# Loading Q and K in 1 MB transfers of 512 B rows, in place of 512 KB transfers of 1 KB rows

## The chip, the cores and the metric

The kernel runs on one core of a Trainium2 chip; the other cores are idle. The metric is the device time of one execution in microseconds, fast runs compared with fast runs (a run is called slow when it lies over 1.5% above the fastest of the same kernel). Ratios are to the kernel before, measured beside each run on the same chip, with a 95% interval in brackets. A profiled execution is shown beside it: its span, from the first to the last instruction, is some 2 us shorter than the time of the execution.

## The reference

Cross-covariance attention over 8 x 12 heads of 512 tokens by 64 channels, all in float32. The attention matrix is 64 x 64 for each head, a product over the tokens:

```python
Q_norm = Q / (np.linalg.norm(Q, axis=-2, keepdims=True) + 1e-10)
K_norm = K / (np.linalg.norm(K, axis=-2, keepdims=True) + 1e-10)
attn = np.einsum('bhnd,bhne->bhde', Q_norm, K_norm)
attn = np.exp(attn - np.max(attn, axis=-1, keepdims=True))
attn = attn / (np.sum(attn, axis=-1, keepdims=True) + 1e-10)
return np.einsum('bhnd,bhde->bhne', V, attn)
```

Two facts matter here. Each of Q, K, V and the output is 12.58 MB, so 50.33 MB cross between HBM and SBUF whatever the kernel does. And Q and K enter only through a sum over tokens: any order of the tokens will do for them, if it is the same for both. The order of V is that of the output.

## The kernel before

A unit is four heads, and there are 24 units. Partition p owns tokens 4p to 4p+3 of each head, 1 KB in one piece (T = 4, D = 64, HU = 4). Every transfer has 512 KB, and all are issued by SyncE.

```python
Qf = Q.rearrange("b h (p t) d -> p (b h) t d", p=128)      # K, V and the output alike
qp = ctx.enter_context(tc.tile_pool(name="qp", bufs=5))    # for Q and K each; vp: 5
LOAD_AHEAD = 3
STORE_LAG = 6

def load_qk(u):
    qf[u] = qp.tile([128, HU, T, D], F32, name="qf")
    kf[u] = qp.tile([128, HU, T, D], F32, name="kf")
    nc.sync.dma_start(out=qf[u], in_=Qf[:, u * HU:(u + 1) * HU])
    nc.sync.dma_start(out=kf[u], in_=Kf[:, u * HU:(u + 1) * HU])
# ... load_v, store; casts to bf16 (VectorE), the products q.k, q.q and k.k of a head in one
#     128 x 128 block, norms, exp, the product with V ...
for u in range(LOAD_AHEAD):
    load_qk(u)
    load_v(u)
# ...
for s in range(U + 2):
    if s + LOAD_AHEAD < U:
        load_qk(s + LOAD_AHEAD)
        load_v(s + LOAD_AHEAD)
    if 0 <= s - STORE_LAG:
        store(s - STORE_LAG)
    # ... grams(s), norms(s), logits(s - 1), exps(s - 1), vtrans(s), casts(s + 1), outs(s - 2)
```

## Time and profile before

| | before |
|---|---|
| time, median of 2 runs | 144.87 us (144.48 to 145.25) |
| span of the profiled run | 143.1 us |
| moved by the DMA engines | 50.49 MB, 353 GB/s in the mean |
| VectorE, TensorE, ScalarE busy | 71%, 67%, 45% of the span |
| data packets | 49,152 of 1,024 B |

The prediction below shows the lines that carry this reading. In all such lines the span is cut into 40 slices, a digit of the DMA row is the busy share in tenths, and the engines are PE (TensorE's matmuls), PEld (its weight loads), DVE (VectorE), ACT (ScalarE), POOL (GpSimd) and SP (SyncE). A packet is one record of a DMA engine's work. One view more: the issues of transfers (what is written and read, the issuing queue, the count, the size, and the median time from issue to landing in us):

```profile
qf<-in_Q_dram SPq DMA_DIRECT2D x24, 512.0 KB, 8.3
kf<-in_K_dram SPq DMA_DIRECT2D x24, 512.0 KB, 8.4
vf<-in_V_dram SPq DMA_DIRECT2D x24, 512.0 KB, 8.4
out_dram<-so SPq DMA_DIRECT2D x24, 512.0 KB, 7.9
```

A transfer of 512 KB at 353 GB/s is 1.5 us of work, yet takes 8 us to land: by an estimate from these two (8.3 / 1.5) some five transfers queue ahead of it. The DMA engines always have work (9 tenths or more in 38 of the 40 slices), and the kernel goes at the pace of their packets.

### The profile page before, as it was taken

The page shows a single profiled execution, that of the slowest core. Times are in us where ns is not written, and L with a number is a line of the kernel's source. Part 1 is how long each engine was busy: PE and PEld are TensorE (multiplying, and loading weights), DVE is VectorE, ACT ScalarE, POOL GpSimd, SP SyncE. Part 2 cuts the span into 40 slices and gives each one's busy share as a digit, 9 for nine tenths or more (in the row PEclk, how much of TensorE's full clock was granted, in tenths as well). Part 3 has the DMA queues.
Part 4 walks back from the last instruction along what each step waited for, and adds up shares of the span by engine and source line. Part 5 has one row for each costly group of instructions (what it writes and reads, how often), then busy time and mean ns, then how long its engine had stood idle before and what let it go on. Part 6 is the DMA issues. An engine that isn't in the chain of part 4 may idle for free.

```text
span 143.1 us, 2715 instructions
## 1 busy us (share of the span) xinstructions
PE 95.3 (67%) x864; PEld 83.7 (59%) x864; DVE 100.9 (71%) x432; ACT 64.8 (45%) x193; POOL 29.9 (21%) x39
## 2 busy tenths in 40 slices
PE   0245879775896797686559874776795694397820
PEld 0234669664795686575557763765694683397620
DVE  0435888989888987696786886883868868767410
ACT  3003406764377644715706536437074273371840
POOL 6003302332033330311302303302022032031100
PEclk9999999999559856857975589655559559855555
DMA  4999999999999999999999999999999999999993
GB/s 133 336 353 349 348 348 351 350 348 348 348 350 348 376 370 378 368 371 384 368 372 380 372 376 379 371 380 371 375 369 369 371 382 372 382 377 386 377 322 113
DMA packets 50701, 50.49 MB, mean 353 GB/s; under 512 B 1536, under 2 KB 50688, under 8 KB 50688
## 3 DMA queue, kind: packets, MB, share of 16 engines
q1 hardware_dynamic: 50688, 50.34, 104.5%
q8 instruction: 6, 0.10, 0.3%
q14 instruction: 7, 0.06, 0.1%
HBM read 37.75 MB, written 12.58 MB: 352 GB/s over the span
## 4 chain that ended last, share of the span: by engine, by line
DMA 65%; DVE 14%; SPq 12%; PE 2%; ACT 1%; issue 1%; ACTq 0%
DMA vf<-in_V_dram 59%; DMA qf<-in_Q_dram 6%; SPq L65 5%; DVE vb L84 4%; SPq L66 4%; DVE ab L134 4%; SPq L70 3%; DVE scr L100 3%; DVE kqs L111 2%; PE lg L119 2%; ACT ex L125 1%; DVE rinv L131 1%; PE po L153 0%; ACT so L154 0%; DVE qkb L78 0%
## 5 line engine op out<-in xcount | busy, mean ns | idle before, releaser
L92 PE MATMUL gram<-qkb 128*128 128x128 bf16 x384 | 39.6, 283 | 20.0 <-DVE qkb L80 19.4
L105 POOL TENSOR_TENSOR rq<-nsq,mhalf 128x4 f32<-128x4 f32 x24 | 27.6, 1151 | 102.0 <-DVE nsq L100 102.0
L92 PEld LDWEIGHTS <-qkb 128*128 128x128 bf16 x384 | 33.8, 130 | 25.3 <-DVE qkb L80 24.6
L125 ACT ACTIVATE ex<-lg,rq 128x64 f32<-128x64 f32 x48 | 14.7, 310 | 63.2 <-PE lg L119 63.2
L119 PE MATMUL lg<-eye,kqs 128*128 128x64 f32 x96 | 22.8, 381 | 19.4 <-DVE kqs L111 19.3
L119 PEld LDWEIGHTS lg<-eye,kqs 128*128 128x128 f32 x96 | 18.8, 271 | 24.9 <-DVE kqs L111 24.9
L145 ACT COPY vt<-vps 128x512 bf16<-128x512 bf16 x48 | 25.7, 593 | 8.7 <-PE vps L143 8.7
L84 DVE CAST vb<-vf 128x1024 bf16<-128x1024 f32 x24 | 16.7, 694 | 15.2 <-DMA vf<-in_V_dram 15.2
L154 ACT COPY so<-po 128x512 f32<-128x512 f32 x48 | 26.4, 618 | 0.3 <-PE po L153 0.3
L143 PE MATMUL vps<-identb,vb 128*128 128x128 bf16 x192 | 20.9, 274 | 1.9 <-DVE vb L84 1.9
L153 PE MATMUL po<-ab,vt 128*128 128x128 bf16 x192 | 20.9, 274 | 0.6 <-DVE ab L134 0.6
L143 PEld LDWEIGHTS <-vb 128*128 128x128 bf16 x192 | 19.3, 138 | 2.2 <-DVE vb L84 2.2
L80 DVE CAST qkb<-kf 128x512 bf16<-128x512 f32 x24 | 10.2, 424 | 11.6 <-DMA kf<-in_K_dram 11.6
L153 PEld LDWEIGHTS <-vt 128*128 128x128 bf16 x192 | 17.4, 129 | 0.9 <-DVE ab L134 0.9
L134 DVE SCALAR_TENSOR_TENSOR ab<-ex,rinv,blocks 128x128 bf16<-128x128 f32 x48 | 14.7, 349 | 0.9
L111 DVE SCALAR_TENSOR_TENSOR kqs<-gram,rq,blocks 128x128 f32<-128x128 f32 x48 | 14.5, 344 | 0.0
L78 DVE CAST qkb<-qf 128x512 bf16<-128x512 f32 x24 | 10.2, 425 | 5.1 <-DMA qf<-in_Q_dram 5.1
L100 DVE CUSTOM_DVE_ANT_0 scr<-gram,swap 128x128 f32<-128x128 f32 x48 | 13.7, 286 | 0.0
L100 DVE CUSTOM_DVE_ANT_0 scr<-gram,ident 128x128 f32<-128x128 f32 x48 | 13.6, 284 | 0.0
L79 DVE CAST qkb<-qf 128x512 bf16<-128x512 f32 x24 | 10.1, 420 | 0.0
L81 DVE CAST qkb<-kf 128x512 bf16<-128x512 f32 x24 | 10.1, 419 | 0.0
L125 ACT ACTIVATION_READ_ACCUMULATOR ex<-lg,rq 128x1 f32 x48 | 9.4, 196 | 0.0
(18 smaller groups left out, 15.8 us busy)
## 6 DMA issues: line engine op xcount, KB each, us to landing
qf<-in_Q_dram SPq DMA_DIRECT2D x24, 512.0 KB, 8.3
kf<-in_K_dram SPq DMA_DIRECT2D x24, 512.0 KB, 8.4
vf<-in_V_dram SPq DMA_DIRECT2D x24, 512.0 KB, 8.4
out_dram<-so SPq DMA_DIRECT2D x24, 512.0 KB, 7.9
```

Source lines behind the costliest of these rows:

```text
L84: nc.vector.tensor_copy(w.rearrange("p t h d -> p h t d"), vf[u])
L92: nc.tensor.matmul(o, x, x, start=(t == 0), stop=(t == T - 1))
L100: nc.vector.tensor_tensor_reduce(out=scr, in0=blk, in1=m, scale=1.0, scalar=1e-20, op0=ALU.mult, op1=ALU.add, accum_out=n2[:, c, p:p + 1],)
L105: nc.gpsimd.tensor_tensor(out=r, in0=n2, in1=mhalf, op=ALU.pow)
L111: nc.vector.scalar_tensor_tensor(out=kk[:, p], in0=gram[u][:, p, 0::3, :], scalar=rq[u][:, 1, p:p + 1], in1=off_diag, op0=ALU.mult, op1=AL ...
L119: nc.tensor.matmul(l[:, p, :], kqs[u][:, p].rearrange("p a d -> p (a d)"), eye2)
L125: nc.scalar.activation(e[:, p, :], lg[u][:, p, :], AF.Exp, scale=rq[u][:, 0, p:p + 1], accum_out=s[:, p:p + 1])
L134: nc.vector.scalar_tensor_tensor(out=a[:, p], in0=e[:, p, None, :].to_broadcast([128, 2, D]), scalar=ri[:, p:p + 1], in1=on_diag, op0=ALU. ...
L143: nc.tensor.transpose(ps[:, t, :], vb[u][:, t, 2 * p:2 * p + 2, :].rearrange("p h d -> p (h d)"), identb)
L145: nc.scalar.copy(w, ps)
L153: nc.tensor.matmul(po[:, t], vt[u, p][:, t, :], ab[u][:, p].rearrange("p a d -> p (a d)"))
L154: nc.scalar.copy(s[:, 2 * p:2 * p + 2].rearrange("p h t d -> p t h d"), po)
```

## The change

The intent: the 512 B rows of neighbouring partitions lie next to each other in HBM (partition p gets tokens 2p and 2p+1, and the same again 256 tokens later), which is meant to let the reads of four neighbours join to 2 KB. If they did, the number of packets for Q and K would be halved, and with it the constant of about 9 ns for each that the prediction estimates from the trace. Q and K come for two units at a time, in 1 MB, with three pairs of buffers for five single ones, and all loads are issued one unit further ahead. The rows of V and the output are left alone.

```diff
-    Qf = Q.rearrange("b h (p t) d -> p (b h) t d", p=128)
-    Kf = K.rearrange("b h (p t) d -> p (b h) t d", p=128)
+    Qf = Q.rearrange("b h (j p t) d -> p (b h) j (t d)", p=128, t=2)
+    Kf = K.rearrange("b h (j p t) d -> p (b h) j (t d)", p=128, t=2)
...
-    qp = ctx.enter_context(tc.tile_pool(name="qp", bufs=5))
+    qp = ctx.enter_context(tc.tile_pool(name="qp", bufs=3))
...
-    LOAD_AHEAD = 3
+    LOAD_AHEAD = 4
...
     def load_qk(u):
-        qf[u] = qp.tile([128, HU, T, D], F32, name="qf")
-        kf[u] = qp.tile([128, HU, T, D], F32, name="kf")
-        nc.sync.dma_start(out=qf[u], in_=Qf[:, u * HU:(u + 1) * HU])
-        nc.sync.dma_start(out=kf[u], in_=Kf[:, u * HU:(u + 1) * HU])
+        if u % 2:
+            return
+        q = qp.tile([128, 2, HU, T, D], F32, name="qf")
+        k = qp.tile([128, 2, HU, T, D], F32, name="kf")
+        heads = slice(u * HU, (u + 2) * HU)
+        nc.sync.dma_start(out=q.rearrange("p u h (j t) d -> p (u h j) (t d)", t=2), in_=Qf[:, heads].rearrange("p h j x -> p (h j) x"))
+        nc.sync.dma_start(out=k.rearrange("p u h (j t) d -> p (u h j) (t d)", t=2), in_=Kf[:, heads].rearrange("p h j x -> p (h j) x"))
+        for i in range(2):
+            qf[u + i], kf[u + i] = q[:, i], k[:, i]
...
-    for u in range(LOAD_AHEAD):
+    for u in range(0, LOAD_AHEAD, 2):
         load_qk(u)
         load_v(u)
+        load_v(u + 1)
```

## The prediction

> **What bounds the kernel now.** I read the page from the totals downward. First the traffic and the queues, part two's last lines and part three:
>
> ```profile
> DMA  4999999999999999999999999999999999999993
> GB/s 133 336 353 349 348 348 351 350 348 348 348 350 348 376 370 378 368 371 384 368 372 380 372 376 379 371 380 371 375 369 369 371 382 372 382 377 386 377 322 113
> DMA packets 50701, 50.49 MB, mean 353 GB/s; under 512 B 1536, under 2 KB 50688, under 8 KB 50688
> q1 hardware_dynamic: 50688, 50.34, 104.5%
> HBM read 37.75 MB, written 12.58 MB: 352 GB/s over the span
> ```
>
> From the second slice to the third from the end the 16 DMA engines are at 9 tenths or more, and the page's share is above 100% because neighbouring packets overlap a little. VectorE is busy 71% and TensorE 67%, so neither fills the span. The bytes are fixed by the problem: Q, K, V and the output are 12.58 MB each. Of 50,688 packets 1,536 are under 512 B: these are the completion counts, 16 for each of 96 transfers. The other 49,152 carry 1 KB each: in each head a partition owns four tokens of 256 B.
>
> Next the chain that ended last, to see whether transfers really set the end:
>
> ```profile
> DMA 65%; DVE 14%; SPq 12%; PE 2%; ACT 1%; issue 1%; ACTq 0%
> ```
>
> 65% is time from an issue to its landing. The 14% on VectorE is where the chain steps back from a cast to the previous transfer; as the DMA engines do not pause there, it isn't a separate cost. Then the traffic in stretches that I chose: loads alone, loads with stores, and the end (columns: length, then busy time and count for PE, PEld, DVE, ACT, POOL, then the granted clock, DMA share and GB/s):
>
> ```profile
> 8.00:42.00 34.00, 24.71 (x231) 21.87 (x230) 28.07 (x122) 15.94 (x48) 8.73 (x7) 0.91 1.10 349
> 46.00:120.00 74.00, 52.74 (x473) 46.60 (x474) 56.55 (x242) 34.33 (x104) 14.46 (x13) 0.68 1.09 374
> 130.00:136.00 6.00, 4.79 (x32) 4.26 (x32) 3.28 (x18) 3.84 (x14) 1.01 (x1) 0.50 1.07 380
> 136.00:143.10 7.10, 1.03 (x8) 0.77 (x8) 0.35 (x2) 1.54 (x3) 0.00 (x0) 0.50 0.62 214
> ```
>
> Loads alone run at 349 GB/s, the mix at 374, stores alone at 380. Per engine, 16 x 1,024 B divided by these is 46.9, 43.8 and 43.1 ns per 1 KB packet. The transfers end within a few us of the last computation, so the kernel is at the rate of its packets almost from start to end.
>
> **What one packet costs.** In the packet records the median 1,024 B packet takes 46 ns and the median 4 B packet 9 ns. A straight line through both has a slope of 37 ns per 1,020 B, 36.3 ns per KB, and a constant of about 9 ns per packet. This line decides the prediction; it assumes that the two sizes sit on one line.
>
> [...] The trace of before shows no joining: there, too, the 1 KB rows of neighbouring partitions are adjacent in a head, and still all data packets are 1,024 B. [...]
>
> **The change, part by part.** (1) Each Q and K transfer becomes two units long: 24 transfers of 1 MB in place of 48 of 512 KB. V and the output stay. The completion packets fall from 96 x 16 to 72 x 16, so 24 per engine at 9 ns: 0.2 us saved. (2) SyncE's first issues[...] took 0.43 to 0.51 us for 512 rows. At the same cost per row the new 2,048 rows take 2.0 us. All together 24 x 2.0 + 48 x 0.5 = 72 us of issue, below the span: not the bound, though only a factor of two away. (3) Token order within Q and K changes in the same way for both, and the product sums over tokens: no compute changes. Every compute engine keeps its order and count of instructions; SyncE has 72 DMA instructions in place of 96. (4) Start: Q(0) was cast at 4.32 us and V(0) at 9.34; now 2 MB come ahead of the first V. At 349 GB/s that extra 1 MB is 3 us. The DMA engines aren't idle meanwhile, so this is absorbed as long as the tail is covered. (5) Tail: behind the last load now stand 11 stores, was 10: 11 x 524 KB at 380 GB/s is 15.2 us. The old last load landed at 128.77 us and the last eviction ended near 137.9, 9 us later, so the stores still cover it: 0 to 0.5 us, either sign. (6) Buffers: three pairs for Q and for K, in place of five units each, and V keeps five while being asked for one unit earlier. [...] the median landing of 8.3 us says that the engines have over 8 us of work queued. I count no new idle time. So all parts but one sum to 0 within 0.5 us; the packets of Q and K decide.
>
> **Branch A, rows of 512 B are what an engine pays for.** A packet is 9.4 ns + 508 B x 0.0363 = 27.8 ns, so 55.7 ns per KB against 46. Q and K are 24,576 KB, 1,536 KB for each engine: 1,536 x 9.7 ns = 14.9 us more, 159.8 us. This is the upper end[...]. Between them I expect some 154.
>
> **Branch B, reads join to 2 KB and a joined read is one packet.** A packet is 46 + 1,024 B x 0.0363 = 83.2 ns against 92 for two: 8.8 ns saved for each 2 KB, 768 times per engine: 6.8 us, 138.1 us. But the mix with stores runs at 43.8 ns per KB already, so some overhead is hidden there. If the load-only third gains fully (8.8 of 92 is 10% of the Q and K two thirds of 40 us: 2.6 us) and the rest half (Q and K half of 90 us, 5%: 2.2 us), 4.8 us is gained: 140 us.
>
> **The rivals.** The two branches are each other's rival. For B speaks that the change is plainly built on it: Q and K alone change, whose token order is free, while V must match the output's rows[...]; and 512 B is chosen where 1 KB was at hand. Against B speaks that the trace has no joining in the same arrangement at 1 KB, so it would need a limit on row size that nothing here shows[...]. Third, the reads join while each 512 B write still pays: then the saving and the cost cancel, and 143 to 147 us follows. [...] Fourth, longer transfers alone, fewer completions and deeper queues: worth 0.2 us by the sum, for the engines are never idle. Fifth, SyncE becomes the bound: if a row costs more to issue in this form than now, up to 150 us or more, and the DMA row would show gaps.
>
> **Range and chances.** I give branch A (with the fifth rival) somewhat under one half, since packet cost is measured here and joining is not; branch B somewhat over a third; the cancelling case the rest. The distribution has two humps, about 140 and about 154. I put the time between them, at 146 us, as the median and not as the likeliest value, with 138 to 158 as the range for 8 in 10. Faster by over 2% (under 142.0 us) has 0.36, within 2% 0.18, slower (over 147.8 us) 0.46.
>
> **What would show it.** The packet count decides most. Branch A: Q and K as 49,152 packets of 512 B, with V and output 24,576 of 1 KB and 1,152 completions, 74,880 in all; traffic in the load-only stretch falls to about 310 GB/s. Branch B: 12,288 packets of 2 KB and so about 38,000 in all; loads alone at 370 GB/s or more. The third: 74,880 packets again, yet an unchanged rate. The fifth: DMA tenths below 9, with 2 us or longer issues of Q and K end to end. If the start or tail was mis-sized, the last store would be issued long before its eviction ended, and the final slices would be low for longer than the present two. What would make the whole wrong: an HBM effect of 512 B reads at 64 KB steps, which no view of this kernel can show, or a stall of V's five buffers, seen as SyncE waiting for the casts of V with the DMA row dipping.

Passages that rest on rules or figures which no trace of this case shows are cut, here and in one expectation below, and the cuts are marked. One of them held a term of the sum: the lower end of branch A, worked out with a smaller constant per packet that was not measured here. Its upper end stands (144.9 + 14.9 = 159.8 us), and "some 154" is between the two. The forecast as a whole came to 146 us in the median, with 138 to 158 for 8 in 10.

## The result

The changed kernel is correct and slower: 160.88 us (160.22 to 161.55, 2 runs) against 144.87. The ratio is 1.1108 (95% interval 1.0997 to 1.1219). A ratio here is always the mean time of one kernel's fast runs over the mean of the other's in the same rounds, so it isn't quite the ratio of the medians that are quoted.

These lines of the changed kernel's page answer to the first ones that the prediction shows:

```profile
DMA  3999999999999999999999999999999999999995
GB/s 99 307 314 311 289 334 290 310 322 290 327 296 295 333 290 324 380 310 304 355 329 300 365 349 293 349 367 293 339 374 296 324 389 309 310 385 385 382 368 188
DMA packets 38029, 50.49 MB, mean 319 GB/s; under 512 B 1152, under 2 KB 25728, under 8 KB 38016
...
q1 hardware_dynamic: 38016, 50.34, 103.1%
...
HBM read 37.75 MB, written 12.58 MB: 318 GB/s over the span
```

Three things are to be seen. The reads did join: between the counts under 2 KB and under 8 KB lie 38,016 - 25,728 = 12,288 packets, in the records all of 2,048 B, as many as the intent asks for. The DMA engines are as busy as ever, with no gap. And yet the rate falls from 353 to 319 GB/s, alternating between about 290 and 380. So it isn't waiting that was added: the same engines, always at work, move the bytes more slowly.

Next the traffic in stretches, for loads alone, loads with stores, and the last two (columns as in the prediction: length, busy time and count of five engines, granted clock, DMA share, GB/s):

```profile
8.00:42.00 34.00, 22.33 (x196) 20.68 (x196) 23.00 (x100) 12.06 (x38) 6.83 (x6) 0.90 1.07 308
46.00:120.00 74.00, 47.35 (x460) 43.58 (x460) 52.89 (x232) 33.61 (x103) 14.66 (x13) 0.71 1.06 329
...
140.00:150.00 10.00, 7.59 (x74) 6.97 (x72) 7.91 (x37) 5.97 (x21) 2.22 (x2) 0.71 1.09 384
150.00:158.00 8.00, 0.76 (x8) 0.53 (x8) 0.78 (x3) 2.04 (x5) 0.00 (x0) 0.66 0.82 283
```

Loads alone fall from 349 to 308 GB/s and the mix from 374 to 329, while the stores at the end go at 384, as before. The loss sits where Q and K are loaded. The chain that ended last, and the issues:

```profile
DMA 55%; SPq 14%; DVE 14%; PE 9%; issue 1%; ACT 1%; POOLq 1%; ACTq 0%
...
vf<-in_V_dram SPq DMA_DIRECT2D x24, 512.0 KB, 8.0
out_dram<-so SPq DMA_DIRECT2D x24, 512.0 KB, 7.1
qf<-in_Q_dram SPq DMA_DIRECT2D x12, 0.5 KB, 9.3
kf<-in_K_dram SPq DMA_DIRECT2D x12, 0.5 KB, 11.7
```

The chain is still mostly transfers. The 0.5 KB for Q and K is what this view makes of a joined transfer; their bytes are in the totals above, which are unchanged. In the packet records the 2,048 B packets take 113.8 ns in the mean and 116 in the median, where the prediction's straight line has 83. About 12 in 100 do take 84 to 90 ns. The change thus brought the packets of the prediction's branch B at the price of branch A.

### The profile page after: what moved, and what is told of

Same layout as the page of the kernel before. It is cut to its first block, busy times and chain, and to the rows that moved or that the text cites. A ratio compares the mean times of both kernels' runs of the same rounds, so it can differ in the third digit from the quotient of the medians.

```text
span 158.1 us, 2695 instructions
## 1 busy us (share of the span) xinstructions
PE 92.3 (58%) x864; PEld 85.0 (54%) x864; DVE 100.0 (63%) x432; ACT 64.8 (41%) x193; POOL 29.5 (19%) x39
## 2 busy tenths in 40 slices
DMA packets 38029, 50.49 MB, mean 319 GB/s; under 512 B 1152, under 2 KB 25728, under 8 KB 38016
## 3 DMA queue, kind: packets, MB, share of 16 engines
q1 hardware_dynamic: 38016, 50.34, 103.1%
## 4 chain that ended last, share of the span: by engine, by line
DMA 55%; SPq 14%; DVE 14%; PE 9%; issue 1%; ACT 1%; POOLq 1%; ACTq 0%
DMA vf<-in_V_dram 55%; SPq L71 7%; SPq L77 5%; DVE vb L91 4%; DVE ab L141 4%; PE lg L126 4%; PE vps L150 3%; DVE kqs L118 2%; PE po L160 2%; SPq L70 2%; DVE scr L107 2%; PE gram L99 1%; POOLq L241 1%; DVE rinv L138 1%; DVE qkb L85 0%
## 5 line engine op out<-in xcount | busy, mean ns | idle before, releaser
L99 PE MATMUL gram<-qkb 128*128 128x128 bf16 x384 | 42.2, 294 | 44.5 <-DVE qkb L87 44.5
L99 PEld LDWEIGHTS <-qkb 128*128 128x128 bf16 x384 | 36.3, 137 | 47.9 <-DVE qkb L87 47.1
L126 PEld LDWEIGHTS lg<-eye,kqs 128*128 128x128 f32 x96 | 19.6, 281 | 16.9 <-DVE kqs L118 16.9
L160 PE MATMUL po<-ab,vt 128*128 128x128 bf16 x192 | 19.3, 259 | 1.0 <-DVE ab L141 1.0
L160 PEld LDWEIGHTS <-vt 128*128 128x128 bf16 x192 | 16.1, 121 | 1.2 <-DVE ab L141 1.2
```

Of the source, the lines that this page charges most:

```text
L99: nc.tensor.matmul(o, x, x, start=(t == 0), stop=(t == T - 1))
L126: nc.tensor.matmul(l[:, p, :], kqs[u][:, p].rearrange("p a d -> p (a d)"), eye2)
L160: nc.tensor.matmul(po[:, t], vt[u, p][:, t, :], ab[u][:, p].rearrange("p a d -> p (a d)"))
```

## The experiments

Three theories were to be told apart. **W**: what an engine pays for is each piece that it writes, and a joined packet has one read of 2 KB but four writes of 512 B, as its four rows go to four partitions. By the straight line four such pieces are 111 ns. **G**: the descriptors of such a transfer are supplied too slowly for all engines together, and an engine waits inside the packet. **R**: the memory is slow to read 2 KB pieces in steps of 64 KB. The first four runs and the kernel before them shared one chip (before: 144.68 us there).

### rows1k_1mb: the size of the transfers alone

```diff
-    Qf = Q.rearrange("b h (j p t) d -> p (b h) j (t d)", p=128, t=2)
+    Qf = Q.rearrange("b h (p t) d -> p (b h) (t d)", p=128)          # K alike
...
+        nc.sync.dma_start(out=q.rearrange("p u h t d -> p (u h) (t d)"), in_=Qf[:, heads])
```

> The change's 1 MB transfers, buffers and order, but rows of 1 KB as before, so only the size of the transfers is tested. Every theory that blames the rows (W: each 512 B piece that is written costs an engine about 29 ns, four of them in a joined packet; G: the descriptors of such transfers are supplied too slowly, at about 1.4 ns each for all engines together, and the engines wait inside the packet; R: the memory is slow to read 2 KB pieces in steps of 64 KB) expects 144 to 146 us and data packets of 1,024 B with a median of 46 ns. If the 1 MB transfers or the three pairs of buffers carry part of the loss, it lies above 147.

Measured: 146.11 us, ratio 1.0095 (1.0039 to 1.0151), correct: 0.11 us above the 144 to 146 that was expected, and under the 147 from which the transfers would have been blamed. Its data packets are of 1,024 B again, with a median of 46 ns. The same two stretches:

```profile
8.00:42.00 34.00, 23.04 (x228) 21.11 (x229) 26.53 (x117) 13.68 (x43) 7.03 (x6) 0.95 1.10 348
46.00:120.00 74.00, 50.46 (x489) 46.56 (x487) 56.52 (x244) 36.62 (x111) 16.31 (x14) 0.71 1.09 369
```

So 1 MB transfers, three pairs of buffers and the new order of issues cost 1.4 us by themselves. They bring nothing, and they are not the cause of the 16 us. Where the 1.4 us goes was not isolated. The load-only stretch has the old 348 GB/s, the mix 369 where before had 374; over 74 us that is about 1 us, so longer runs of loads between stores are the likely place, but that is only argued.

### rows2k_flat: the same packets, written in one piece

```diff
+    Qf = Q.rearrange("b h n d -> (b h n) d").rearrange("(g p t) d -> p g (t d)", p=128, t=8)   # K alike
...
+        rows = slice(u * HU // 2, (u + 2) * HU // 2)
+        nc.sync.dma_start(out=q.rearrange("p u (g i) t d -> p (u g) (i t d)", i=2), in_=Qf[:, rows])
```

> Wrong result on purpose: each partition takes 2 KB in one piece (eight tokens, so two heads are mixed), 1 MB transfers. Packets of 2,048 B as in the change, but written in one piece. W and G: the packet takes 83 to 85 ns, and the time falls to 138 to 141 us, the prediction's branch B. R: the packet stays at 110 ns or more and the time near 160 us, as reads of 2 KB are what is slow.

Measured: 139.32 us, ratio 0.9631 (0.9565 to 0.9697); the result is wrong (relative error 0.044). The traffic and packet lines of its page:

```profile
GB/s 93 395 366 378 380 361 387 360 379 377 364 386 357 380 376 383 396 391 380 399 398 373 395 401 374 390 403 372 390 408 382 389 406 386 384 385 385 384 373 82
DMA packets 38029, 50.49 MB, mean 369 GB/s; under 512 B 1152, under 2 KB 25728, under 8 KB 38016
```

The packet line agrees with the changed kernel's number for number except the mean rate: 369 GB/s, was 319. The 2 KB packets take 84 ns in the median and 87.1 in the mean. The count of packets is therefore not what decides; the same 12,288 packets are worth -5 us when each is written in one piece and +16 us when it is written in four. This is branch B of the prediction: 139.32 us lies between its 138.1 for the full saving and its 140.

### rows512_apart: 512 B rows that don't join

```diff
+    Qf = Q.rearrange("b h (p j t) d -> p j (b h) (t d)", p=128, j=2)     # K alike
...
+        for dst, src in ((q, Qf), (k, Kf)):
+            for j in range(2):
+                nc.sync.dma_start(out=dst.rearrange("p u h (j t) d -> p j (u h) (t d)", j=2)[:, j], in_=src[:, j, heads])
```

> 512 B rows that cannot join: a partition owns 1 KB of a head as before, and its two halves come in two transfers of 512 KB, so neighbouring rows of a transfer are 512 B apart in memory. 49,152 packets of 512 B. W: 27 to 30 ns each, the same cost for each KB as in the change, so 157 to 163 us. G, where a read descriptor counts like a write descriptor: 4,096 descriptors for 1 MB at 1.4 ns are 5.8 us, against 3.6 in the change, so 190 us or more. R: anything from 160 up, with no number.

Measured: 161.23 us, ratio 1.1169 (1.1079 to 1.1259), correct. From its page:

```profile
DMA packets 75279, 50.52 MB, mean 313 GB/s; under 512 B 1536, under 2 KB 75264, under 8 KB 75264
```

75,264 - 24,576 - 1,536 = 49,152 packets of 512 B, none joined, of 27 to 36 ns for 8 in 10 of them (median 32; the profiled run was the longest of the four, 163.25 us). Four times as many reads for Q and K as in the changed kernel, half the size of before's, and the time is that of the changed kernel (161.23 against 160.88). The joining of reads is worth nothing here. G in the form that counts a read like a write is out: it asked for 190 us.

### two_queues: packets of V and the output always at hand

```diff
-        nc.sync.dma_start(out=vf[u], in_=Vf[:, u * HU:(u + 1) * HU])
+        nc.scalar.dma_start(out=vf[u], in_=Vf[:, u * HU:(u + 1) * HU])
...
-        nc.sync.dma_start(out=Of[:, u * HU:(u + 1) * HU], in_=so[u])
+        nc.scalar.dma_start(out=Of[:, u * HU:(u + 1) * HU], in_=so[u])
```

> The change with the V loads and the stores issued from ScalarE's queue, so that the engines have packets of both kinds at hand all the time. G: an engine that has no descriptor of Q or K ready serves V or a store in the meantime, the 2 KB packets fall to 84 ns in the median, and the time to 137 to 145 us. W: an engine is itself busy with the four pieces, nothing is hidden, packets stay near 116 ns and the time within 157 to 163 us. R: in between, 145 to 157.

Measured: 163.13 us, ratio 1.1272 (1.1195 to 1.1348), correct. The total can't be read as W's 157 to 163, because it has a second cause. The DMA row of its page:

```profile
DMA  4999999999999999999999999999999999533796
```

and four stretches of it, columns as above:

```profile
10.00:44.00 34.00, 19.91 (x190) 18.20 (x191) 22.04 (x100) 10.95 (x34) 6.00 (x5) 0.95 1.08 309
46.00:120.00 74.00, 45.23 (x431) 41.95 (x432) 49.63 (x219) 29.50 (x89) 14.37 (x12) 0.74 1.07 351
...
93.90:97.30 3.40, 2.61 (x23) 2.61 (x24) 3.40 (x17) 1.56 (x4) 1.21 (x1) 0.68 1.06 381
...
134.00:148.00 14.00, 9.64 (x128) 8.10 (x127) 13.38 (x65) 9.29 (x30) 4.58 (x4) 1.00 0.53 183
```

From 134 to 148 us the DMA engines are half idle: the stores now stand in ScalarE's own order of work, and from 131 to 148 us one is issued every 4 us. By an estimate from the two rates that costs 14 us x (1 - 183/384) = 7.3 us; without it the time would be near 156.

What answers the question for loads is the load-only stretch: 309 GB/s, no more than the 308 of the changed kernel, although 1 KB packets of V were queued beside them (a V transfer landed 13.5 us after its issue in the median, where the changed kernel had 8.0). The 2 KB packets do get shorter there, 109 ns in the mean for 117 in the changed kernel, but the 1 KB packets get longer by as much, 62 for 53. The pair takes what it took, so V's loads did not fill the extra time.

Stores did fill it. The packets of ScalarE's queue were given to its transfers by counting 512 for each in the order of issue; that they run in this order is assumed. Where a store runs beside loads of Q and K (nine stretches with over 200 of their packets; of each transfer the middle nine tenths), the 2 KB packets have a median of 87 to 91 ns, the stores' own one of 46 to 47, and the rate is 354 to 387 GB/s; the stretch from 93.9 to 97.3 us above is one of them. Beside V they take 109 ns in the median stretch. So W does not hold as it was put: the engine is not itself busy for all of the 116 ns (102 was the median over the whole run, where W said near 116). It handled stores in the meantime, and another load it did not. The mix as a whole ran at 351 GB/s for the changed kernel's 329. What the second queue is worth in total this run's end hides.

### probe_alone: the transfers by themselves

Before the untouched kernel come nine transfers into one scratch tile. Each starts when VectorE has read from the tile that the one ahead filled. The sources are views of Q (written short; `probe` stands for the transfer and the read behind it):

```diff
+    Qj = Q.rearrange("b h (j p t) d -> p (b h j) (t d)", p=128, t=2)   # 512 B rows; Qs: t=1; Qw: 1 KB, (p t)
+    Qc = Q.rearrange("b h (j p t) d -> p (b h j) (t d)", p=32, t=8)    # 2 KB chunks
+    probe(Qj[:, 0:32])                        # 1: 128 partitions x 32 rows
+    probe(Qj[0:127, 32:36])                   # 2: 127 partitions x 4 rows
+    probe(Qw[:, 20:36])                       # 3: 1 KB rows, 128 x 16
+    probe(Qw[0:127, 36:38])                   # 4: 1 KB rows, 127 x 2
+    probe(Qs[:, 160:192])                     # 5: 256 B rows, 128 x 32
+    probe(Qc[:, 100:108])                     # 6: into partitions 0, 4, 8, ...
+    probe(Qj[:, 110:126], Qj[:, 126:142])     # 7: from two queues
+    probe(Qj[0:40, 142:174])                  # 8: 40 partitions x 32 rows
+    probe(Qj[:, 180])                         # 9
```

> The kernel of before with nine transfers in front of it, each alone: it starts only when the one ahead has landed. What is read are their packets and rates, the total time is of no interest. (1) 2 MB in 512 B rows that join, on all engines: 116 to 118 ns for each 2 KB packet and 285 to 295 GB/s, as in the change. (2) The same rows on 127 partitions[...]. W (each piece costs the engine that writes it): 110 to 118 ns again. A limit that the engines share (supply of descriptors, memory, fabric): 84 ns, as one engine alone doesn't reach it. (3) and (4), the same pair with 1 KB rows: W 46 to 47 ns in both; shared: 47 in (3) and at most 46 in (4). (5) 256 B rows: W, pieces of 9.4 + 9.2 ns, 75 ns for a packet of 1 KB if four rows join and 149 if eight do, 210 to 220 GB/s; a supply of 1.8 ns for each piece: 140 GB/s. (6) The 2 KB chunks of (1), written in one piece to every fourth partition: W and supply 84 ns; memory: 116. (7) As (1), but half from each of two queues: a supply that is counted for each queue gives 84 ns; W, memory or a common supply 116. (8) 40 partitions[...]: W 110 to 118 ns; shared: 84 to 90.

The count of engines is here an estimate from the completion packets: 16 for 128 partitions, one for 127 and ten for 40. With 127 partitions the DMA share was 0.07 and 0.06 in the stretches of (2) and (4), about one engine of 16. The packets of each transfer, from the packet records (a step is the time from one packet's start to the next on one engine, late in the transfer; for several engines it is worked out from their joint rate; the times of packets overlap a little, so a packet can take longer than the step):

| | pieces written | data packets | ns for one packet | by the prediction's line |
|---|---|---|---|---|
| 1 | 512 B, all engines | 1,024 of 2,048 B | first 84, then 118.9 in the mean, step 113 | 4 x 27.8 = 111 |
| 2 | 512 B, one engine | 508 of 512 B | 33 median, step 27.1 | 27.8 |
| 3 | 1 KB, all engines | 2,048 of 1,024 B | 46 median, step 46.8 | 46 |
| 4 | 1 KB, one engine | 254 of 1,024 B | 46 median, step 45.9 | 46 |
| 5 | 256 B, all engines | 1,024 of 1,024 B | early 52 to 64, late 86, step 75 | 4 x 18.5 = 74 |
| 6 | 2 KB, all engines | 256 of 2,048 B | 84 median | 83 |
| 7 | 512 B, two queues | 1,024 of 2,048 B | 116 median, step 113 | 111 |
| 8 | 512 B, ten engines | 1,280 of 512 B | early 28, late 60, step 46 | 27.8 |

Two of these can be seen in the transfer view. First transfer 1, in 40 slices of a quarter microsecond:

```profile
DMA  0000000888989999999999999999999999983000
GB/s 0 0 0 0 0 0 0 96 129 201 297 345 337 329 345 281 305 313 289 265 313 289 289 273 305 289 289 273 305 297 281 289 289 297 281 241 89 0 0 0
```

About 340 GB/s for a microsecond, then 290 to the end. After the start-up the packets take 84 ns, as long as the 2 KB packets of transfer 6 that are written in one piece, up to about the thirteenth of each engine; the later ones take 118.9 in the mean. Why the first ones are faster the trace does not show. I read the 84 ns as one read of four rows, and not as four reads put down as one packet: four single 512 B packets of transfer 2 take longer, 4 x 22 = 89 ns at its start, where they come fastest (23 GB/s in the view below), and 4 x 27 = 108 later. The margin at the start is small. Then transfer 2:

```profile
GB/s 0 4 12 1 9 23 21 23 21 19 19 19 19 20 19 19 20 19 19 19 19 20 19 19 19 20 19 19 19 19 20 19 19 19 20 19 19 19 13 0
DMA packets 509, 0.26 MB, mean 17 GB/s; under 512 B 1, under 2 KB 509, under 8 KB 509
```

One completion packet and 508 rows at 19 GB/s: a single engine, with no other transfer beside it. Its step of 27.1 ns for a 512 B piece, times four, is 108 of the 113 ns of transfer 1's step. So almost all of the cost is there without sharing. My expectation had the rows of this transfer join; they didn't, and the piece's own step answers as well.

Transfers 6 and 7 speak against the others. Transfer 6 reads the same 2 KB chunks at the same 64 KB steps and writes each in one piece: 84 ns. It is short, 16 packets for each engine, but its last two still take 84 ns where the same ones of transfer 1 take about 115. So R falls, as it did in rows2k_flat with steps of 256 KB. In transfer 7 the packets take 118 to 119 ns while both queues are at work, so a supply that is counted for each queue falls too. In transfer 5 the step is 75 ns, or 218 GB/s, where W said 75 and 210 to 220; a supply of 1.8 ns for each piece would have given 140 GB/s. Its mean of 76.1 ns over all packets mixes faster early ones with late ones of 86.

Transfer 8 is a miss for everybody: its rows did not join, and late in it a piece costs a step of 46 ns, where one engine alone needs 27. So the piece's own cost is not the only limit there is. Why is open.

### rows512_512k: the rows alone, with the transfers of before

```diff
-        nc.sync.dma_start(out=qf[u], in_=Qf[:, u * HU:(u + 1) * HU])
+        heads = slice(u * HU, (u + 1) * HU)
+        nc.sync.dma_start(out=qf[u].rearrange("p h (j t) d -> p (h j) (t d)", t=2), in_=Qf[:, heads].rearrange("p h j x -> p (h j) x"))   # K alike
```

(With the change's Qf and Kf, and all else as before.)

> The joining rows of 512 B alone, in transfers of 512 KB with the buffers and the order of before. All theories that blame the rows expect 157 to 162 us and 12,288 packets of 2 KB at 110 to 120 ns in the median. If part of the loss comes from the 1 MB transfers together with these rows, it is under 155.

Measured: 159.80 us, ratio 1.1071 (1.1022 to 1.1120), correct, on another chip, where before took 144.46.

```profile
DMA packets 75277, 50.49 MB, mean 320 GB/s; under 512 B 1536, under 2 KB 75264, under 8 KB 75264
```

The time is as expected, the packets aren't: at 8 rows for each partition nothing joined, 49,152 packets of 512 B. So the joining came with the 1 MB transfer of 16 rows; and by the time it made no difference (159.80 us without it, 160.88 with it). The rows alone cost 15.3 us (159.80 - 144.46); with rows1k_1mb's 1.4 us for the rest, that is 16.7, against the measured 16.0.

Taken together: the loss follows the pieces that are written, joined in the reading or not, and not the size of the transfers, the count of packets or the steps in HBM. That stores filled the time and V's loads didn't (two_queues: 87 to 91 ns for a 2 KB packet beside a store, 109 beside V) says that the time is not spent by the whole engine. Which part of the work on a piece takes it was not shown.

When rows joined is only known case by case. Four rows of neighbouring partitions joined with 128 partitions and 16 or 32 rows of 512 B (to 2 KB: 12,288 packets in the changed kernel, 1,024 each in transfers 7 and 1) and with 32 rows of 256 B (to 1 KB: 1,024 packets in transfer 5). They did not join with 8 rows of 512 B (this run), with 16 rows of 1 KB (2,048 packets of 1,024 B in transfer 3), on 127 partitions with 4 rows (508 packets of 512 B in transfer 2), or on 40 with 32 rows (1,280 of 512 B in transfer 8). What decides it is open.

### rows2k_right: a version from what was learned

The rows of rows2k_flat put one head in partitions 0 to 63 and the next in 64 to 127. With products over 64 partitions the result is right:

```diff
+        t_ = qkb[u] = qkp.tile([128, PU, 2 * T, 3 * D], BF16, name="qkb")
+        nc.vector.tensor_copy(t_[0:D, :, :, 0:D], qf[u][0:D])
+        nc.vector.tensor_copy(t_[D:128, :, :, 2 * D:3 * D], qf[u][D:128])
+        nc.vector.tensor_copy(t_[:, :, :, D:2 * D], kf[u])
...
+        for p in range(PU):
+            for t in range(2 * T):
+                for i in range(2):
+                    o = g[:, i, p]                      # one bank for each i
+                    x = qkb[u][D * i:D * i + D, p, t, D * i:D * i + 2 * D]
+                    nc.tensor.matmul(o, x, x, start=(t == 0), stop=(t == 2 * T - 1))
```

> A version that should beat both, with a right result: the 2 KB rows of rows2k_flat, in which partitions 0 to 63 hold one head and 64 to 127 the next, so that the products are taken over 64 partitions each (16 matmuls for two heads, was 8, in two banks), and Q is cast in two halves of 64 partitions. W: pieces of 2 KB, packets at 84 ns, and 138 to 142 us as in rows2k_flat, if TensorE and VectorE keep up. If TensorE doesn't (twice the matmuls in the line that is its longest), 145 us or more, with gaps in the DMA row.

(Not shown: two PSUM pools go from two buffers to one, as the tile of the products grows from 2 to 4 KB for each partition.) Measured, on a third chip: correct, and faster than both kernels. The three fast runs took 139.94 to 141.14 us, 140.67 in the median, ratio 0.9707 (0.9616 to 0.9798) to before at 144.73. Two of the five runs were slow, the profiled one among them (145.26 us). Its packets are those that rows2k_flat had in the fast state: 12,288 of 2,048 B, 84 ns in the median. It is within 2 us of what the wrong-result kernel reached. Whether the remainder is TensorE's, which now has 1,248 matmuls in place of 864, or comes from the single PSUM buffers, a profile in the fast state would have to show.

## Why the prediction was wrong

**Bound and line were right, and branch A's sum nearly.** The kernel was and is at the pace of its packets, with no idle DMA engine. The constant per packet and the slope, read off before's 4 B and 1,024 B packets, held for pieces of 256, 512 and 2,048 B alone within a few ns (steps of 75 ns for 74 worked out and 27.1 for 27.8, packets of 84 for 83); transfer 8 is the exception, with a step of 46 for 27.8. Branch A's upper end, 14.9 us for the rows, stands against 15.3 measured for the rows alone. Its working has a slip: it puts 9.4 ns for the first 4 B, though the median it read was 9. With 9 a 512 B packet is 27.4 ns, and the branch ends at 158.5 us. (The "36.3 ns per KB" are for 1,000 B.)

**The first step that failed** is in branch A: "Between them I expect some 154." I took the line's 14.9 us down to 9 for the sake of a smaller constant per packet, though the trace had already given about 9 ns. The measured figure should have decided. The range then ended at 158, under the branch's own upper end of 159.8 and under the 160.88 that was measured.

**The second** is what the branches were built on: that the joining of packets decides ("The packet count decides most."). The count was that of branch B, 38,016, and the time that of branch A. The line's cost followed the pieces written, as rows2k_flat (one piece, 139.32 us) and rows512_apart (no joining, 161.23 us) show from both sides. The third rival had the mechanism, joined reads with each 512 B write still paid, but its size, "then the saving and the cost cancel", was wrong. Even the prediction's own sizes, 6.8 us saved and up to 14.9 us of cost, don't cancel. Its sign was wrong as well: "74,880 packets again, yet an unchanged rate" is neither the count that came nor the rate, 308 GB/s for 349. It added a saving on reads to a cost on writes. In the trace of the transfer alone a joined packet took 84 ns early on and 118.9 afterwards, at a step of 113, which is that of four single pieces (4 x 27.1 = 108) and a little more. So the saving is nil: 160.88 us with joined reads, 161.23 without.

**The third, smaller,** is "So all parts but one sum to 0 within 0.5 us": the parts other than the rows cost 1.4 us (rows1k_1mb).

**The rest.** Issue was no bound, as predicted, though 2.0 us for the first Q transfer was off: it took 0.84. The load-only rate of branch A was given as about 310 GB/s, and 308 was measured. The start's 3 us came as worked out, with V(0) cast at 12.32 us for 9.34. The fourth rival, 0.2 us gained by longer transfers, was tested by rows1k_1mb and lost 1.4 us; the fifth and the HBM effect were not seen. SyncE did wait longer for V's buffers, 29.8 us for 17.2, but the DMA row did not dip. Why loads alone run slower than loads mixed with stores, 349 against 374 GB/s in the kernel before, with stores alone at 380, is open.

## What to carry to other kernels

Count the pieces on both sides of a transfer, the read and the write: joining reads was worth nothing here while the writes stayed in pieces of 512 B (160.88 us joined, 161.23 not). The time that they cost was filled by stores from another queue (87 to 91 ns for a 2 KB packet beside a store, for 116 in the changed kernel), but not by V's loads (309 GB/s, for 308 in the changed kernel); a version that uses this, with its stores issued in time, was not run. A line through two packet sizes of the kernel at hand (here 9 ns for 4 B, 46 ns for 1 KB) gave the cost of other sizes within a few ns, on one engine (27.1 ns for 27.8) and on all 16 (113 for 111); trust it before a figure that was not measured on the kernel, and do not average the two. What gained here was a piece that is long within a partition (2 KB in one piece: 84 ns, and 140.67 us in rows2k_right), though that spreads two heads over the halves of the partitions.
